# Operands loaded straight into their split buffers, and state space rows in two blocks of 512 columns around the memory tiles

## The chip, the core and the metric

The kernel runs on one core of a Trainium2 chip. The metric is the time of one execution on the device in microseconds (us). A core has a matrix engine (TensorE, PE in the profile; PEld is its weight load), a vector engine (VectorE, DVE), a scalar engine (ScalarE, ACT), a general engine (GpSimd, POOL) and a synchronising engine (SyncE, SP), each with its own instruction queue that is worked off in order. Data moves between the memory of the chip (HBM, "DRAM" in the code) and the on-chip buffers by DMA; this kernel issues its loads on SP's queue and its stores on POOL's. Matmuls write to PSUM, which has eight banks of 128 x 512 float32.

## The reference

One layer of a streaming encoder with 1024 tokens and 1024 features, all in float32. It is three sub-layers, each normalised before and after and added to its input. The change touches the first and the start of the second.

```python
h = rms_norm(x, mix_pre_g)
proj = h @ w_in                       # 512 columns u, 3 x 512 columns q, k, v, 8 gates
y_ssm = s5_mixer(u, ...)              # state space branch, then gelu and a gate
y_fox = forgetting_attention(q, k, v, f_logit)   # 8 heads x 64, causal
y_mix = concatenate([rms_norm(y_ssm, ssm_out_g), rms_norm(y_fox, fox_out_g)])
x = x + rms_norm(y_mix @ w_out, mix_post_g)
h = rms_norm(x, xa_pre_g)
x = x + rms_norm(memory_cross_attention(h, mem_n, xa_wq, xa_wkv, xa_wo), xa_post_g)
h = rms_norm(x, ffn_pre_g)
x = x + rms_norm((silu(h @ w_gate) * (h @ w_up)) @ w_down, ffn_post_g)
```

The cross-attention reads 256 memory tokens (`mem`), with 4 heads of 256; keys and values are `rms_norm(mem) @ xa_wkv`.

## The kernel before

**Products in three parts.** Float32 operands are split into a high part, rounded to the format that PE multiplies fast, and a low part, the rest. `split` (lines 112 to 119) makes both: ACT copies the source to the high part, DVE subtracts it from the source to make the low part. `mm3` (lines 121 to 124) then does three matmuls per product: high x high, high x low, low x high. A weight is loaded into a staging buffer (tag `raw`, two of them, or tag `e`) and split into a pair of tiles (tag `whl`, three of them) by `load_w` (line 154).

**Buffers.** A tag names a set of buffers that are handed out in turn: `slab` (16 of 8 KB per partition), `raw` (2), `whl` (3), `a` (2), `b` (2), `c` (3), `d` and `e` (1 each), `t2` (3 small ones), `yt` (2). A tile's writer waits until the buffer's last user is done. PSUM has four banks tagged `g`; the other four are `s` during attention and `x` behind it.

**Order.** The kernel is traced in Python with generators that hand over to each other, and a scheduler then sets the order of each queue from a model of the times, with priorities by the order of tracing. `tc.issue_after(i)` keeps what is traced inside it behind instruction `i` on that instruction's engine. Nothing is reordered on the chip: a wait at the head of a queue holds what stands behind it.

**Stages.**

1. `in_proj` (line 869): the projections of u, keys, values and queries. Its last part interleaves `v1`, the second half of the value tiles (8 tiles of 24 matmuls), with `ssm_out`, which turns states to outputs; the tuple `V1_AT` says how many value tiles go before each of its steps. Remaining value tiles move on to the next stage.
2. Attention (`fox`, line 705) has 8 heads x 8 query tiles; `paced` takes one step of side work (`fillers`, line 975) behind each of its steps. The side work is in this order: remaining value tiles, the gate (`glu`), one step of the state space rows (`out_ssm`, line 818), the load and split of the memory tokens with five more row steps, sixteen memory tiles (`mem_tile`: one block of 128 columns of `xa_wkv` each, stored to `kv_d`), the remaining rows, and the first two heads' keys times query weights (`build_a(0)`, line 993).
3. `out_ssm` multiplies the state space branch by the upper half of `w_out`, for all 1024 rows, in four blocks of 256 columns. Each block has one split weight tile. Each tile of 128 rows has 4 x 3 matmuls, an evacuation scaled by `r_s` on ACT (line 836), and one store to `t1_d` for two of them (line 840). Its first block computes the row scales (`glu_stats`).
4. Behind attention, lines 1023 to 1082: the lower half of `w_out` is loaded (`raw`) and split into four slabs (line 1026). For each of eight row tiles the kernel loads x (tag `c`, line 1060) and the half result of stage 3 from `t1_d` in two pieces (tags `a`, `a`, `b` in turn, line 1063), multiplies the attention output by the weights, adds the half result (line 1070), squares, scales and adds x (line 1078). `value_weights(0)` and `(1)`, the values times output weights of two memory heads, go between the half tiles. Their values come from `kv_d` through a `t2` buffer (line 1035) into a split tile with tag `b` or `e`.
5. `build_a(1)` and `value_weights(2)` and `(3)`, then the cross-attention and the feed-forward part, which the change doesn't touch.

Of the kernel before, what the change touches and what calls it, by code (L numbers as in the profile page):

```python
# [17 lines left out]
P = 128  # L18
S = 1024
D = 1024  # L20
# [14 lines left out]
MAGIC = 12582912.0  # L35
RATE = 1.02
HP = 16 * (L - 1)
V1_AT = (3, 1, 1, 1, 1)
HID = ("11", "12", "22", "S1", "S2", "S3", "S4")
EVB = 13  # L40
OPB = 10
# [11 lines left out]
def layer(ctx: ExitStack, tc: tile.TileContext, a, out):  # L53
# [24 lines left out]
    def g_ps(shape):  # L78
        return psg.tile(shape, F32, name="g", tag="g")
# [41 lines left out]
    def mm3(ps, lh, ll, rh, rl, first, last):  # L121
        pe.matmul(ps, lh, rh, start=first, stop=False)  # L122
        pe.matmul(ps, lh, rl, start=False, stop=False)  # L123
        pe.matmul(ps, ll, rh, start=False, stop=last)  # L124
# [21 lines left out]
        return last, done  # L146

    boost = 5000
    stA, stB, stC = pool, pool, pool

    def tables(name):
# [2 lines left out]
    def load_w(src, shape, first=0, stage=None):  # L154
        w = tt(stage, [P, D]) if stage else raw([P, D])
        hl = whl([P, 2, D])
        if not first:
            sp.dma_start(out=w, in_=src)
        for cs in (slice(0, first), slice(first, D)):
            if cs.start < cs.stop:  # L160
                if first:
                    sp.dma_start(out=w[:, cs], in_=src[:, cs])
                with tc.high_priority(offset=boost):
                    split(hl[:, 0, cs], hl[:, 1, cs], w[:, cs])
        v = hl.rearrange("p t (a b) -> p t a b", b=shape)
        return v[:, 0], v[:, 1]
# [15 lines left out]
    nc_d = dram.tile([NH, S], F32, name="nc_d")  # L182
    t1_d = dram.tile([L, NC, D], F32, name="t1_d")
    kv_d = dram.tile([16, P, 256], F32, name="kv_d")
    x1_d = dram.tile([NT, P, D], F32, name="x1_d")
    x2_d = dram.tile([NT, P, D], F32, name="x2_d")
    t_d = dram.tile([8, P, 4, 512], F32, name="t_d")
# [7 lines left out]
    def tt(tag, shape=None, dt=F32):  # L195
        return t4.tile(shape or [P, S], dt, name=tag, tag=tag, bufs=BUFS[tag])

    def t2t(shape, dt=F32):
        return tt("t2", shape, dt)
# [616 lines left out]
        rsqrt_mean(r_f, sv, 512)  # L816

    def out_ssm(ys):
        for cc in range(4):
            wh, wl = load_w(a["w_out_s"][cc], 256, stage="e" if cc == 2 else None)  # L820
            for j0 in range(0, NT, 2):
                o = t2t([P, 2, 256])
                made = []
                for j in range(j0, j0 + 2):
                    ts = slice(j * P, (j + 1) * P)
                    ps = g_ps([P, 256])
                    for k in range(4):
                        mm3(ps, ys[k][:, 0, ts], ys[k][:, 1, ts], wh[:, k], wl[:, k], k == 0, k == 3)
                    made.append((j, ps))
                    if cc + j0 == 0:  # L830
                        yield
                        if j == 0:
                            continue
                        glu_stats()
                    for jj, ps in made:
                        act.activation(out=o[:, jj - j0], in_=ps, func=AF.Copy, scale=r_s[:, jj:jj + 1])
                    made = []
                    if j == j0:
                        yield
                stB.dma_start(out=t1_d.rearrange("j c d -> c j d")[:, j0:j0 + 2, cc * 256:cc * 256 + 256], in_=o)  # L840
                yield

    def drain(*gens):
# [25 lines left out]
    def in_proj():  # L869
        r_mem.append(mem_stats())  # L870
        yield from k4
        for i in range(1, 4):
            yield from qk_tile(i + 4, xH, xL, rb)
        for n, _ in enumerate(v_tiles(0, xH, xL, r_x)):
            if n % 2:
                yield
        f_gate(gate[0])
        for i in range(4):
            yield from qk_tile(i, xH, xL, rb)
        drain(gs)  # L880
        go = ssm_out()
        for n in V1_AT:
            step(v1, n)
            step(go)
        drain(go)
# [89 lines left out]
    def fillers():  # L975
        yield from v1
        yield from glu(ys)
        mem = []
        rows = out_ssm(ys)
        step(rows)  # L980
        yield
        for _ in mem_load(r_mem[0], mem):
            step(rows)
            yield
        for i in range(16):
            mem_tile(i, *mem)
            yield
        yield from rows
        yield from build_a(0)
# [3 lines left out]
    def build_a(c):  # L993
        for t in range(2):
            Ah[c, t], Al[c, t] = slab([P, 4, 512]), slab([P, 4, 512])
        for h in range(2):
            hd = 2 * c + h
            kr = t2t([P, 2, 256])
            sp.dma_start(out=kr, in_=kv_d[2 * hd:2 * hd + 2].rearrange("d p m -> p d m"))
            kh = tt(("ea", "ba")[c][h], [P, 2, 2, 256], F32R)  # L1000
            split(kh[:, 0], kh[:, 1], kr)
            wq = [load_w(a["wqT"][2 * hd + d], P) for d in range(2)]
            ms = slice(h * 256, h * 256 + 256)
            for ft in range(0, KT, 2):
                ps = g_ps([P, 2, 256])
                for f in range(2):
                    for d in range(2):
                        mm3(ps[:, f], wq[d][0][:, ft + f], wq[d][1][:, ft + f], kh[:, 0, d], kh[:, 1, d], d == 0, d == 1)
                for f in range(2):
                    split(Ah[c, ft // 4][:, ft % 4 + f, ms], Al[c, ft // 4][:, ft % 4 + f, ms], ps[:, f],  # L1010
                          g_xa[:, ft + f:ft + f + 1])
                yield
# [9 lines left out]

    wo = []
    for i in range(4):
        w = raw([P, D])
        sp.dma_start(out=w, in_=a["w_out_f"][i])
        hl = slab([P, 2, D])
        split(hl[:, 0], hl[:, 1], w)
        wo.append(hl)
    g_mp = gain_row(0, "d")  # L1030
    VW = {}

    def value_weights(h):
        vr = t2t([P, 2, 256])
        sp.dma_start(out=vr, in_=kv_d[8 + 2 * h:8 + 2 * h + 2].rearrange("d p m -> p d m"))
        vh = tt("bebe"[h], [P, 2, 2, 256], F32R)
        split(vh[:, 0], vh[:, 1], vr)
        wo_ = [load_w(a["wo"][2 * h + d], 512) for d in range(2)]
        for mt in range(2):
            VW[2 * h + mt] = slab([P, 2, D])  # L1040
        for c in range(2):
            tiles = [(mt, (x_ps if h == 3 else g_ps)([P, 512])) for mt in range(2)]
            for d in range(2):
                for mt, ps in tiles:
                    ms = slice(mt * P, mt * P + P)
                    mm3(ps, vh[:, 0, d, ms], vh[:, 1, d, ms], wo_[d][0][:, c], wo_[d][1][:, c], d == 0, d == 1)
                    yield
            for mt, ps in tiles:
                split(VW[2 * h + mt][:, 0, c * 512:c * 512 + 512], VW[2 * h + mt][:, 1, c * 512:c * 512 + 512], ps)
# [6 lines left out]
    kept = {}  # L1056
    for n, j in enumerate((3, 4, 5, 6, 7, 0, 1, 2)):
        ts = slice(j * P, (j + 1) * P)
        xt = tt("c")
        sp.dma_start(out=xt, in_=a["x"][ts, :])  # L1060
        t = tt("aab"[n % 3])
        for i in range(2):
            sp.dma_start(out=t[64 * i:64 * i + 64], in_=t1_d.rearrange("j (k s) d -> s k j d", s=16)[2 * j + i])
        ss4, ss, r = sm(4, "ss4"), sm(1, "ss"), sm(1, "r")
        for h in range(2):
            hs = slice(h * 512, h * 512 + 512)
            ps = x_ps([P, 512])
            for k in range(4):
                mm3(ps, yf[k][:, 0, ts], yf[k][:, 1, ts], wo[k][:, 0, hs], wo[k][:, 1, hs], k == 0, k == 3)
            dve.scalar_tensor_tensor(out=t[:, hs], in0=ps, scalar=r_f[:, j:j + 1], in1=t[:, hs], op0=ALU.mult, op1=ALU.add)  # L1070
            for q in range(2 * h, 2 * h + 2):
                act.activation(out=tt("yt", [P, 256]), in_=t[:, q * 256:q * 256 + 256], func=AF.Square,
                               accum_out=ss4[:, q:q + 1])
            pool.tensor_tensor(out=t[:, hs], in0=t[:, hs], in1=g_mp[:, hs], op=ALU.mult)
            step(between)
        dve.tensor_reduce(out=ss, in_=ss4, op=ALU.add, axis=mybir.AxisListType.X)
        rsqrt_mean(r, ss, D)
        dve.scalar_tensor_tensor(out=xt, in0=t, scalar=r, in1=xt, op0=ALU.mult, op1=ALU.add)
        if j < 3:
            kept[j] = xt  # L1080
        else:
            stC.dma_start(out=x1_d[j], in_=xt)
# [489 lines left out]
def lay_out(i):  # L1572
# [11 lines left out]
    def kt(g):  # L1584
# [16 lines left out]
        "ssm_dcol": i["ssm_d"].reshape(4, P).T,  # L1601
        "glu_w": i["ssm_glu_w"].reshape(2, 2, P, 512).transpose(0, 2, 1, 3),
        "glu_b": kt(i["ssm_glu_b"]),
        "w_out_s": i["w_out"][:512].reshape(4, P, 4, 256).transpose(2, 1, 0, 3),
        "w_out_f": i["w_out"][512:].reshape(4, P, D),
        "wkv": cols(i["xa_wkv"]),
        "wqT": i["xa_wq"].T.reshape(8, P, D),
# [21 lines left out]
```

## Time and profile before

| | |
|---|---|
| median of 3 runs | 1413.33 us (1409.28 to 1413.37) |
| the profiled execution | 1414.33 us, span of its instructions 1412.5 us |
| mean granted clock of TensorE | 0.992 |
| PE busy | 1381.8 us (98% of the span) |
| DVE, ACT, POOL busy | 951.9, 652.3, 379.7 us |
| DMA | 239.45 MB, mean 170 GB/s |
| PE without work, 235 to 300 us | 5.1 us of 65 |
| PE without work, 300 to 460 us | 0 of 160 |
| PE without work, 460 to 580 us | 9.0 us of 120 |

An engine is busy from the start to the end of its instructions. Matmuls overlap, so their printed durations add up to more than PE's time, and PE's rate is read from the distance of their starts. "<-" in a row means "written from", and in brackets behind a row stand the idle time before it and what ended it. L122 is line 122 of the kernel. SPq rows are SP's DMA issues. The half results, `t1_d`, appear as `t_d` in the rows.

### The profile page before, as it was taken

Reading aid. Unit: us, or ns where it says so; the run is one execution under the profiler, and the core shown is the slowest. Engines: PE = TensorE matmul, PEld = TensorE weight load, DVE = VectorE, ACT = ScalarE, POOL = GpSimd, SP = SyncE. Lnnn points to the kernel's source line nnn. Section 1 sums busy time; section 2 is a strip of 40 time slices with the busy share of each in tenths; the row PEclk is TensorE's granted clock in tenths of the full one; section 3 lists DMA queues with packets and bytes.
Section 4 is the critical chain, followed back from the end, with each engine's and each line's share of the span. In section 5 each row is a group of like instructions: output and inputs, shape, how many; then the busy total and the mean of one; then the engine's idle time right before and its main releaser. Section 6 shows DMA issues by size and latency. Waiting matters only on the chain.

```text
span 1412.5 us, 20273 instructions
## 1 busy us (share of the span) xinstructions
PE 1381.8 (98%) x7353; PEld 1163.3 (82%) x7353; DVE 951.9 (67%) x1719; ACT 652.3 (46%) x1289; POOL 379.7 (27%) x430
## 2 busy tenths in 40 slices
PE   9999989999999899999999999999999999999997
PEld 7889889789889677888888788888888888888886
DVE  8949944857567668545467777877776676655566
ACT  7383345766566546433344533333333334544351
POOL 0011110011211043001021367676766661000021
PEclk9999999999999999999999999999999999999999
DMA  6235665267663665024467345554444447955544
GB/s 217 91 108 163 201 220 138 69 200 213 183 180 113 175 194 186 27 75 152 161 202 257 97 176 193 178 187 161 145 158 154 165 150 236 357 196 194 179 164 164
DMA packets 104501, 239.45 MB, mean 170 GB/s; under 512 B 11464, under 2 KB 40136, under 8 KB 104272
## 3 DMA queue, kind: packets, MB, share of 16 engines
q1 hardware_dynamic: 85872, 176.24, 40.0%
q0 software_dynamic: 18528, 61.91, 12.3%
q8 instruction: 58, 0.95, 0.3%
q14 instruction: 43, 0.35, 0.1%
HBM read 169.43 MB, written 77.33 MB: 175 GB/s over the span
## 4 chain that ended last, share of the span: by engine, by line
PE 84%; DVE 7%; issue 3%; DMA 3%; ACT 2%; POOL 0%; SPq 0%; DVEq 0%; ACTq 0%; POOLq 0%
PE x L1294 17%; PE g L1294 13%; PE x L1557 7%; PE g L1557 7%; PE g L122 7%; PE g L124 7%; PE g L123 7%; PE x L123 2%; PE x L124 2%; PE g L758 2%; PE x L122 2%; PE g L772 2%; PE s L730 1%; PE s L731 1%; DMA a<-t_d 1%
## 5 line engine op out<-in xcount | busy, mean ns | idle before, releaser
L1294 PE MATMUL x<-slab,op 128*128 128x512 f32 x984 | 233.2, 389 | 0.5 <-DVE op L115 0.5
L1294 PEld LDWEIGHTS x<-slab,op 128*128 128x128 f32 x984 | 184.7, 188 | 39.2 <-DVE op L115 1.0
L1294 PE MATMUL g<-slab,op 128*128 128x512 f32 x744 | 178.7, 389 | 0.0
L115 DVE TENSOR_TENSOR slab<-slab 128x1024 fp32r<-128x1024 f32 (+2 forms) x92 | 110.2, 1207 | 86.4 <-ACT slab L113 85.2
L1294 PEld LDWEIGHTS g<-slab,op 128*128 128x128 f32 x744 | 139.7, 188 | 29.0
L122 PE MATMUL g<-slab,whl 128*128 128x512 f32 (+1 forms) x416 | 151.4, 364 | 0.8 <-ACT slab L485 0.4
L124 PE MATMUL g<-slab,whl 128*128 128x512 f32 (+1 forms) x416 | 148.7, 358 | 0.0
L123 PE MATMUL g<-slab,whl 128*128 128x512 f32 (+1 forms) x416 | 148.3, 357 | 0.0
L113 ACT ACTIVATE slab<-slab 128x1024 fp32r<-128x1024 f32 (+2 forms) x92 | 94.7, 1036 | 108.6 <-DMA slab<-hs_d 80.8
L1557 PE MATMUL g<-slab 128*128 128x512 f32 x462 | 126.6, 389 | 0.0
L1557 PE MATMUL x<-slab 128*128 128x512 f32 x462 | 126.6, 389 | 0.0
L1557 PEld LDWEIGHTS g<-slab 128*128 128x128 f32 x462 | 86.7, 188 | 18.0
L1557 PEld LDWEIGHTS x<-slab 128*128 128x128 f32 x462 | 86.7, 188 | 18.0
L115 DVE TENSOR_TENSOR op<-slab,op 128x512 fp32r<-128x512 f32 x80 | 84.6, 1068 | 11.5 <-ACT op L113 11.3
L1370 POOL TENSOR_TENSOR wt<-wt 128x256 f32<-128x256 f32 x88 | 83.1, 944 | 21.0 <-DMA wt<-in_w_down 17.4
L122 PE MATMUL g<-whl,slab 128*128 128x256 f32 (+2 forms) x288 | 86.8, 310 | 1.7 <-ACT yt L318 0.7
L122 PEld LDWEIGHTS g<-slab,whl 128*128 128x128 f32 x416 | 78.6, 189 | 12.0 <-ACT whl L113 0.6
L124 PEld LDWEIGHTS g<-slab,whl 128*128 128x128 f32 x416 | 78.4, 189 | 11.6 <-DVE whl L115 0.2
L123 PEld LDWEIGHTS g<-slab,whl 128*128 128x128 f32 x416 | 78.6, 189 | 10.6
L113 ACT ACTIVATE op<-slab 128x512 fp32r<-128x512 f32 x80 | 50.0, 628 | 79.9 <-PE g L1294 38.0
L124 PE MATMUL g<-whl,slab 128*128 128x256 f32 (+2 forms) x288 | 86.0, 299 | 0.0
L123 PE MATMUL g<-whl,slab 128*128 128x256 f32 (+2 forms) x288 | 85.7, 298 | 0.0
(397 smaller groups left out, 2890.3 us busy)
## 6 DMA issues: line engine op xcount, KB each, us to landing
hs_d<-ev POOLq DMA_DIRECT2D x77, 256.0 KB, 2.6
slab<-hs_d SPq DMA_DIRECT2D x35, 512.0 KB
wt<-in_w_down SPq DMA_DIRECT2D x44, 256.0 KB
wt_d<-wt POOLq DMA_DIRECT2D x22, 512.0 KB, 5.1
slab<-in_w_gate SPq DMA_DIRECT2D x20, 512.0 KB
slab<-in_w_up SPq DMA_DIRECT2D x20, 512.0 KB
slab<-wt_d SPq DMA_DIRECT2D x20, 512.0 KB
wd_d<-in_w_down SPq DMA_DIRECT2D x33, 256.0 KB
```

Of the source, the lines that this page charges most:

```text
L113: first = act.activation(out=hi, in_=src, func=AF.Copy, scale=1.0 if mul is None else mul)
L115: (lo_eng or dve).tensor_tensor(out=lo, in0=src, in1=hi.bitcast(F32), op=ALU.subtract)
L122: pe.matmul(ps, lh, rh, start=first, stop=False)
L123: pe.matmul(ps, lh, rl, start=False, stop=False)
L124: pe.matmul(ps, ll, rh, start=False, stop=last)
L730: pe.matmul(ps[:, c0:c1], qt, ka[:, 0, c0:c1], start=True, stop=False)
L731: pe.matmul(ps[:, c0:c1], qt, ka[:, 1, c0:c1], start=False, stop=not dg)
L758: pe.transpose(tp[:, k], sc[:, (k0 + k) * P:(k0 + k + 1) * P], ident)
L772: pe.matmul(yp[hh * 64:hh * 64 + 64, c0:], w, pts[2 * hp + hh, qc][:, k, c0:], start=k == 0, stop=k == nk - 1, tile_position=(0, 64 * hh))
L1294: pe.matmul(ps, x[:, k], y[:, k], start=first and k + n == 0, stop=k == 3 and n == 2, skip_group_check=not first)
L1370: pool.tensor_tensor(out=o, in0=x, in1=y, op=ALU.subtract)
L1557: pe.matmul(banks[n][j], xo[:, u, js], wo[:, v], start=ends[0] and k == 0, stop=ends[1] and k == 2, skip_group_check=onto is not None)
```

## The change

- **Rows.** `out_ssm` works in two blocks of 512 columns, each with two split weight tiles, one matmul of 512 columns in place of two of 256, one evacuation and one store per row tile. It hands over twice per row tile, so it has 32 steps (33 before).
- **Order of the side work.** The whole first block (one step and fifteen more) goes with the load of the memory tokens ahead of the sixteen memory tiles; the second block follows them.
- **`V1_AT`** starts with 2 in place of 3: one value tile more is left for attention's side work.
- **In place.** Keys (`build_a`), values (`value_weights`) and the lower half of `w_out` are loaded into the low half of their split tile, which DVE then overwrites with source minus high part. The staging buffers go away there: `t2` for the keys, `raw` for `w_out`. The values' two halves are now two `t2` buffers, in place of a `t2` and a tag `b` or `e`.
- **A copy.** The lower half of `w_out` is copied within HBM to `wof_d` early, on SP behind the last weight load of the keys, and read from there later.
- **Half results and x.** Half results take `a` and `b` in turn (four buffers), x takes `e` for the first and fifth tile and `c` for the others. All loads of x, and the half results of all tiles but the first, are issued behind the last read of `wof_d`.

```diff
-V1_AT = (3, 1, 1, 1, 1)
+V1_AT = (2, 1, 1, 1, 1)
...
     def load_w(src, shape, first=0, stage=None):
...
-            sp.dma_start(out=w, in_=src)
+            fetched.append(sp.dma_start(out=w, in_=src))
...
+    wof_d = dram.tile([4, P, D], F32, name="wof_d")
...
     def out_ssm(ys):
-        for cc in range(4):
-            wh, wl = load_w(a["w_out_s"][cc], 256, stage="e" if cc == 2 else None)
-            for j0 in range(0, NT, 2):
-                o = t2t([P, 2, 256])
-                made = []
-                for j in range(j0, j0 + 2):
-                    ts = slice(j * P, (j + 1) * P)
-                    ps = g_ps([P, 256])
-                    for k in range(4):
-                        mm3(ps, ys[k][:, 0, ts], ys[k][:, 1, ts], wh[:, k], wl[:, k], k == 0, k == 3)
...
-                stB.dma_start(out=t1_d.rearrange("j c d -> c j d")[:, j0:j0 + 2, cc * 256:cc * 256 + 256], in_=o)
+        for c in range(2):
+            ws = [load_w(a["w_out_s"][2 * c + kk], 512) for kk in range(2)]
+            held = []
+            for j in range(NT):
+                ts = slice(j * P, (j + 1) * P)
+                ps = g_ps([P, 512])
+                for k in range(4):
+                    wh, wl = ws[k // 2]
+                    mm3(ps, ys[k][:, 0, ts], ys[k][:, 1, ts], wh[:, k % 2], wl[:, k % 2], k == 0, k == 3)
+                    if k == 1:
                         yield
+                held.append((j, ps))
+                if c + j == 0:
+                    yield
+                    continue
+                if c == 0 and j == 1:
+                    glu_stats()
+                for j_, ps in held:
+                    o = t2t([P, 512])
+                    act.activation(out=o, in_=ps, func=AF.Copy, scale=r_s[:, j_:j_ + 1])
+                    stB.dma_start(out=t1_d[j_][:, c * 512:c * 512 + 512], in_=o)
+                held = []
                 yield
...
         for i in range(1, 4):
             yield from qk_tile(i + 4, xH, xL, rb)
+            if i == 3:
+                with tc.issue_after(fetched[-1].ins):
+                    for j in range(4):
+                        sp.dma_start(out=wof_d[j], in_=a["w_out_f"][j])
...
-        for _ in mem_load(r_mem[0], mem):
+        loads = mem_load(r_mem[0], mem)
+        for _ in range(2 * NT - 1):
+            step(loads)
             step(rows)
             yield
...
-            kr = t2t([P, 2, 256])
+            kh = tt(("ea", "ba")[c][h], [P, 2, 2, 256], F32R)
+            kr = kh[:, 1].bitcast(F32)
             sp.dma_start(out=kr, in_=kv_d[2 * hd:2 * hd + 2].rearrange("d p m -> p d m"))
-            kh = tt(("ea", "ba")[c][h], [P, 2, 2, 256], F32R)
...
-        w = raw([P, D])
-        sp.dma_start(out=w, in_=a["w_out_f"][i])
         hl = slab([P, 2, D])
+        w = hl[:, 1].bitcast(F32)
+        wo_read = sp.dma_start(out=w, in_=wof_d[i])
...
-        vr = t2t([P, 2, 256])
+        vh, vl = t2t([P, 2, 256], F32R), t2t([P, 2, 256], F32R)
+        vr = vl.bitcast(F32)
...
-        vh = tt("bebe"[h], [P, 2, 2, 256], F32R)
-        split(vh[:, 0], vh[:, 1], vr)
+        split(vh, vl, vr)
...
-        xt = tt("c")
-        sp.dma_start(out=xt, in_=a["x"][ts, :])
-        t = tt("aab"[n % 3])
-        for i in range(2):
-            sp.dma_start(out=t[64 * i:64 * i + 64], in_=t1_d.rearrange("j (k s) d -> s k j d", s=16)[2 * j + i])
+        t = tt("ab"[n % 2])
+        with tc.issue_after(wo_read.ins) if n else ExitStack():
+            for i in range(2):
+                sp.dma_start(out=t[64 * i:64 * i + 64], in_=t1_d.rearrange("j (k s) d -> s k j d", s=16)[2 * j + i])
+        xt = tt("ec"[n % 4 > 0])
+        with tc.issue_after(wo_read.ins):
+            sp.dma_start(out=xt, in_=a["x"][ts, :])
...
-        "w_out_s": i["w_out"][:512].reshape(4, P, 4, 256).transpose(2, 1, 0, 3),
+        "w_out_s": i["w_out"][:512].reshape(2, 2, P, 2, 512).transpose(3, 0, 2, 1, 4).reshape(4, P, 1024),
```

More of the change, by code (lines that the diff above doesn't have):

```diff
@@ L148, in layer @@
     boost = 5000
+    fetched = []
     stA, stB, stC = pool, pool, pool
@@ L818, in out_ssm @@
     def out_ssm(ys):
-        for cc in range(4):
-            wh, wl = load_w(a["w_out_s"][cc], 256, stage="e" if cc == 2 else None)
-            for j0 in range(0, NT, 2):
-                o = t2t([P, 2, 256])
-                made = []
-                for j in range(j0, j0 + 2):
-                    ts = slice(j * P, (j + 1) * P)
-                    ps = g_ps([P, 256])
-                    for k in range(4):
-                        mm3(ps, ys[k][:, 0, ts], ys[k][:, 1, ts], wh[:, k], wl[:, k], k == 0, k == 3)
-                    made.append((j, ps))
-                    if cc + j0 == 0:
-                        yield
[L832 to L839, printed above, removed]
-                stB.dma_start(out=t1_d.rearrange("j c d -> c j d")[:, j0:j0 + 2, cc * 256:cc * 256 + 256], in_=o)
+        for c in range(2):
[8 more added lines that the diff above has]
+                    if k == 1:
+                        yield
+                held.append((j, ps))
[9 more added lines that the diff above has]
+                held = []
                 yield
@@ L1045, in value_weights @@
                     ms = slice(mt * P, mt * P + P)
-                    mm3(ps, vh[:, 0, d, ms], vh[:, 1, d, ms], wo_[d][0][:, c], wo_[d][1][:, c], d == 0, d == 1)
+                    mm3(ps, vh[:, d, ms], vl[:, d, ms], wo_[d][0][:, c], wo_[d][1][:, c], d == 0, d == 1)
                     yield
```

## The prediction

> **What bounds the kernel now.** I read the page first (engine shares), then the stretches of the span as a table, then PE's waits, and only at its gaps the order of the instructions, engine by engine.
>
> ```profile
> span 1412.5 us, 20273 instructions
> PE 1381.8 (98%) x7353; PEld 1163.3 (82%) x7353; DVE 951.9 (67%) x1719; ACT 652.3 (46%) x1289; POOL 379.7 (27%) x430
> ```
>
> PE is busy 1381.8 of 1412.5 us, so a change can only shorten PE's work, remove some of its 30.7 us of gaps, or remove the slow clock behind them. The profiled execution took 1414.33 us, 1.8 us more than its span, and the runs shown have a median of 1413.33. I sum against 1414.33 and take 1.0 off at the end. The edits touch what runs between about 105 and 560 us. The gaps there, by stage (columns: stretch, its length, busy time of PE, PEld, DVE, ACT, POOL, the granted clock, DMA share, GB/s):
>
> ```profile
> 190.00:235.00 45.00, 40.54 (x316) 39.41 (x315) 8.16 (x12) 18.41 (x30) 5.55 (x11) 0.92 0.56 169
> 275.00:300.00 25.00, 20.62 (x144) 17.69 (x143) 17.02 (x45) 17.91 (x40) 2.00 (x3) 0.86 0.64 181
> 300.00:365.00 65.00, 65.00 (x535) 59.38 (x533) 41.21 (x79) 37.74 (x74) 9.02 (x16) 1.00 0.63 190
> 485.00:495.00 10.00, 8.46 (x43) 6.34 (x43) 5.06 (x5) 4.92 (x8) 1.72 (x2) 0.83 0.61 191
> 512.00:523.00 11.00, 9.47 (x42) 7.51 (x40) 5.08 (x8) 1.41 (x6) 4.12 (x4) 1.00 0.56 180
> ```
>
> The reader sees two things. From 300 us PE has no gap, so attention's softmax on DVE and ACT is hidden and only PE's own work counts. Elsewhere a gap costs twice: a granted clock of 0.86 over 25 us is 3.5 us of lost work beside the 4.4 us idle, and 0.83 over 10 us is 1.7 us beside 1.5. Who ends the gaps (engine, line, releaser: us, times, longest):
>
> ```profile
> PE g L643 <- ACT t L316: 3.9, 2, 3.3
> PE g L122 <- DVE slab L115: 2.5, 2, 2.0
> PE g L772 <- ACT t L836: 2.4, 1, 2.4
> PE x L122 <- DVE a L1070: 1.9, 1, 1.9
> PE g L758 <- ACT d L782: 1.5, 1, 1.5
> ```
>
> **The wider blocks of state space rows: PE.** The projection of 1024 rows goes from 4x8x4x3 = 384 matmuls of 256 columns to 2x8x4x3 = 192 of 512. What counts is the distance between starts, not the printed duration. Two rows of each width, first and last of an unbroken run (11 and 34 matmuls):
>
> ```profile
> 374.24 0.28 PE L123 MATMUL g<-whl,slab 128*128 128x256 f32 x1
> ...
> 375.43 0.28 PE L124 MATMUL g<-whl,slab 128*128 128x256 f32 x1
> 504.31 0.39 PE L122 MATMUL x<-slab 128*128 128x512 f32 x1
> ...
> 511.79 0.39 PE L122 MATMUL x<-slab 128*128 128x512 f32 x1
> ```
>
> (375.43 - 374.24) / 10 = 0.119 us and (511.79 - 504.31) / 33 = 0.2267 us. So 384 x 0.119 = 45.7 against 192 x 0.2267 = 43.5: **2.2 us less PE work**, in a stage where PE has no gaps, so it counts in full. The Trainium skill (TensorE: Matmul & The Clock Gate, Back-to-back issue gap) gives 2.5 ns on top of the columns for each matmul; by it 192 fewer matmuls are worth an estimated 0.5 us, and the whole sum below would be 1.7 us smaller. The rows show some 12 ns a pair, so the trace doesn't agree, and it decides. On ACT 32 evacuations of 0.47 us become 16 of 512 columns. Their nearest row, a 512-column copy, takes 0.6 to 0.7 us, so ACT saves about 4.7 us, worth nothing by itself beside a PE without gaps. POOL issues as many stores as before.
>
> ```profile
> L836 ACT ACTIVATE t<-g,r_s x32: 450/470/478, 282.3 to 449.9; 128x256 f32<-128x256 f32 x32
> L688 ACT ACTIVATE t<-t x6: 612/617/632, 248.9 to 270.7; 128x512 f32<-128x512 f32 x6
> ```
>
> **The memory tiles move behind the first block.** Before, six row steps and then sixteen memory tiles; after, sixteen row steps, then the tiles. Side work keeps 66 steps, one per attention step. The gap at 287 us:
>
> ```profile
> L115 DVE TENSOR_TENSOR slab<-slab 128x1024 fp32r<-128x1024 f32 (+2 forms) x92 | 110.2, 1207 | 86.4 <-ACT slab L113 85.2
> ...
> 280.12 1.11 SPq L718 DMA_DIRECT2D a<-qk_d  x2
> 281.32 0.53 SPq L158 DMA_DIRECT2D raw<-in_wkv  x1
> 286.22 1.06 ACT L113 ACTIVATE whl<-raw 128x1024 fp32r<-128x1024 f32 x1 [2.22 <-DMA raw<-in_wkv]
> 289.00 0.45 ACT L836 ACTIVATE t<-g,r_s 128x256 f32<-128x256 f32 x1
> 289.51 3.24 PE L772 MATMUL g<-slab 128*64 128x256 f32 x16 [2.37 <-ACT t L836]
> ```
>
> SP is held by attention's query load until 280.12. The first memory weights leave only at 281.32, ACT stands at their split until 286.22, and the evacuation queued behind it releases PE's bank at 289.5. Ten more row steps now lie ahead of that split. The first and the last L836 (282.3 and 449.9, the row above) are 46 steps apart, so a step is 3.6 us and the weights have 36 us more. This takes away 2.4 us and half of this stage's slow-clock loss, 1.7: **-4.1**. The other gap of this stage (1.5 us, L782) hangs on the scale factors, whose place is kept; I leave it and its 1.7, which sets the bounds at 0 and -7.3. In turn block 0 needs two split weight tiles, and the second waits for the gate's weights to be released. A split of 1024 columns is 1.06 us on ACT and 1.2 on DVE (L113 and L115 in the rows), within one step's 3.6: 0, with 2 as the upper bound (no cover).
>
> **One value tile later, V1_AT.** One tile, 24 x 0.119 = 2.9 us, moves into attention's side work; the sum of work stays. The stall there:
>
> ```profile
> 189.63 1.07 POOL L297 DMA_DIRECT2D qk_d<-t  x2 [6.41 <-ACT t L113]
> 198.07 0.47 ACT L316 ACTIVATE t<-g,r_x 128x256 f32<-128x256 f32 x1 [5.92 <-DMA qk_d<-t]
> 198.60 0.80 PE L643 MATMUL g<-slab 128*128 128x128 f32 x2 [3.33 <-ACT t L316]
> ```
>
> The buffer for the second tile's rows comes free when a store issued at 189.63 lands, at 198.07; that isn't moved. PE fills its four banks by then either way. 0; bounds -3.3 (the stall goes) and +2.
>
> **Output weights in place, behind a copy.** The copy is 4 transfers of 512 KB from HBM to HBM, issued on SP after the last key weights (about 101 us). SP is next used at 117.3, and the DMA is empty meanwhile:
>
> ```profile
> 105.00:110.00 5.00, 5.00 (x24) 4.14 (x23) 3.50 (x9) 2.18 (x6) 0.00 (x0) 1.00 0.67 232
> 110.00:115.00 5.00, 5.00 (x29) 4.38 (x28) 5.00 (x11) 1.06 (x1) 0.00 (x0) 1.00 0.00 0
> 100.96 0.80 SPq L158 DMA_DIRECT2D raw<-in_w_f  x2
> 117.30 3.09 SPq L524 DMA_DIRECT2D slab<-slab  x2
> ```
>
> 2 MB at the 232 GB/s of the first row is 9 us: that empty stretch hides it. 0, at most +3 if it slides into the loads of 120 us and later. The reads themselves:
>
> ```profile
> 470.06 3.38 SPq L1060 DMA_DIRECT2D c<-in_x  x2
> 474.52 1.22 SPq L1063 DMA_DIRECT2D a<-t_d  x2
> 475.84 1.23 SPq L1026 DMA_DIRECT2D raw<-in_w_out_f  x2
> 484.41 1.06 ACT L113 ACTIVATE slab<-raw 128x1024 fp32r<-128x1024 f32 x1 [6.41 <-DMA raw<-in_w_out_f]
> ...
> 487.22 2.98 PE L772 MATMUL g<-slab 128*64 128x256 f32 x14 [1.54 <-ACT slab L763]
> ...
> 488.00:489.00 1.00, 1.00 (x9) 0.59 (x6) 0.39 (x1) 0.00 (x0) 0.00 (x0) 0.50 0.80 254
> ```
>
> The last two weights wait for a staging buffer, leave behind two x loads and a half result, and land 8.5 us later. ACT stands at their split for 6.4 us with attention's last evacuations (L763) behind it; PE idles 1.5 us and then has half its clock, 1.7 us of loss. In place they need no staging buffer, and x and all half results but one queue behind them. I take **-3.2**. The Trainium skill (TensorE: Matmul & The Clock Gate, What's actually happening) lets the clock fall after an idle window of about 3.4 us; by it neither this gap nor the one at 287 us costs clock, and the sum below would shrink by 3.4 to -6.2. The last row shows 0.50 right behind a gap of 1.54: the trace does not agree here, so the sum keeps the losses.
>
> **Four buffers for half results; keys and values in place.**
>
> ```profile
> 514.25 3.62 SPq L1063 DMA_DIRECT2D a<-t_d  x4
> 522.53 0.75 DVE L1070 SCALAR_TENSOR_TENSOR a<-x,r_f,a 128x512 f32<-128x512 f32 x1 [5.68 <-DMA a<-t_d]
> ...
> t_d<-t POOLq DMA_DIRECT2D x26, 256.0 KB, 3.2
> ```
>
> A half result leaves at 514.25, when its buffer is free, and lands about 522.5: PE's 1.9 us wait on L1070. With two more choices the load leaves earlier: **-1.9**, or 0 if the queue still holds it. Against it stand the values, which now need two of three small buffers per head, so the second head's load must wait for the first head's products. The load is some 3 us (stores of a like 256 KB land in a median of 3.2), the split about 1.3 by half of the 1024-column rows and their fixed part; half a row tile, 12 x 0.2267 = 2.7 us, covers part. **+1.8**; bounds 0 and 4.5. The keys wait for an attention buffer that is released a head earlier: 0.
>
> **Sum:** -2.2 - 4.1 + 0 + 0 - 3.2 - 1.9 + 1.8 = -9.6; 1414.33 - 9.6 - 1.0 = 1403.7. For gaps that fall elsewhere when five queues are reordered I give back one gap of the kind shown, 1.5 us. **Forecast: 1405 us.**
>
> **The rivals.** *No net change, about 1411.* PE's work falls by 2.2, but the gaps only move: the in-order waits of ACT on a weight split and of DVE on L115 come back at the next load (2.5 us of L122 on L115 stand in the waits). For it: the gaps above end at a wait queued ahead of an unrelated evacuation. Against: DMA is idle or half used around them. *Slower, about 1418: the in-place reads wait for their slabs.* A read into a staging buffer can run ahead; a read into the slab can't leave before attention releases it. If the last slab is one that PE's L772 reads (487.22 + 2.98 = 490.2 in the row above), the read lands 8.5 us later, near 498.7 instead of 484.4, and x and the other half results, tied behind it on SP, later still. PE lacks 14 us of inputs, of which the values' products, 48 x 0.2267 = 10.9, cover half if their own weights are in: 8.5 us idle, 1.7 of clock and 1 for the first half result are +11 in place of -3.2 - 1.9, less the 1.5 and 1.8 already counted: 1405 + 16 - 3 = 1418. It decides once a slab is released later than about 484. Against: rows are worked on from 477 already, so two slabs were free by then. *Larger gain, about 1398:* the scale-factor gap with its clock (-3.2) and the V1_AT stall (-3.3) go too; for it, value tile and evacuations sit in the same queues. *The gaps go, but the clock stays as slow, about 1408:* the slow stretches end and start by themselves and fall on other work; then the 1.7 of the memory term and of the output weights are not won (1405 + 3.4). For it: the 512 to 523 stretch has 1.5 us idle at a clock of 1.00, so a gap need not cost clock. This is also the time by the idle window of the Trainium skill, named above.
>
> **Chances.** Forecast 0.45, clock not won 0.10, larger gain 0.13, no net change 0.19, slower 0.13. Runs within 0.3% (4.2 us) can't be told from no change, so faster means below 1409.1 and slower above 1417.6. Of the forecast 0.03, of the clock case 0.03 and of the slower case 0.01 fall to "same": faster 0.42 + 0.07 + 0.13 = 0.62, same 0.26, slower 0.12. The range runs from just below the larger gain to the slower case's centre: **1396 to 1418**; the forecast's own is 1400 to 1409.
>
> **What would show it.** Right: 192 matmuls of 128x512 at 0.227 us from start to start in the rows; no PE wait on L836 behind a wkv load; 485 to 495 without an idle; no DVE wait of over 2 us on a half result. Wrong: SP's wait ahead of the output weights ends at an attention read and ACT still stands over 5 us at their split; a PE wait at the values' products; PE gaps in 115 to 190.

## The result and the profile after

The changed kernel takes 1417.68 us (median of 6 runs, 1416.81 to 1420.07) against 1409.57 us for the kernel before on the same chip (6 runs, 1405.75 to 1413.37): ratio 1.0055, 95% interval 1.0034 to 1.0075. It is about 8 us slower; 1405 was forecast. The profiled execution took 1418.36 us, its span is 1416.6 us. In the code of the changed kernel, lines up to 145 keep their numbers; behind them L238 is L240, L643 is L645, L763 is L765, L836 is L840, L999 is L1008, L1035 is L1044, L1070 is L1080 and L1078 is L1088. Stretches stand at fixed times, and each edit moves the work by some us against them, so only large differences count.

PE's waits in the changed kernel (engine, line, releaser: us, times, longest):

```profile
PE g L122 <- ACT t L113: 10.8, 1, 10.8
PE g L645 <- DMA slab<-T_d: 2.7, 1, 2.7
PE g L760 <- DVE sv_s L240: 1.8, 1, 1.8
PE g L239 <- ACT slab L765: 1.8, 1, 1.8
PE g L122 <- ACT slab L765: 1.4, 1, 1.4
```

The first is new and is longer than any wait before. By stretch, changed kernel (columns as in the prediction):

```profile
275.00:300.00 25.00, 20.08 (x111) 14.70 (x112) 15.24 (x43) 16.91 (x37) 1.63 (x3) 0.80 0.60 179
485.00:495.00 10.00, 10.00 (x59) 8.36 (x56) 1.77 (x7) 1.37 (x4) 0.74 (x1) 1.00 0.85 204
512.00:523.00 11.00, 10.41 (x46) 8.32 (x45) 9.58 (x18) 6.27 (x23) 6.58 (x6) 1.00 0.92 273
541.00:580.00 39.00, 28.61 (x145) 23.85 (x146) 30.42 (x52) 24.42 (x57) 7.81 (x4) 0.82 0.31 95
```

The last stretch of the kernel before (length, PE busy, granted clock, DMA share, GB/s):

```profile
541.00:580.00 39.00, 35.99 (x192) 0.96 0.39 120
```

The stretch of the output weights, 485 to 495 us, has its full 10 us and full clock. The one at 275 us is no better than before. The loss is behind 541 us: 7.4 us more idle time and a clock of 0.82 in place of 0.96. Read in steps of 0.1 us, the clock is at half from 541.8 to 555.5, but PE has nothing to do until 550.3, so most of that low clock costs no work. The order of events there, engine by engine, in the changed kernel:

```profile
516.26 0.39 SPq L1044 DMA_DIRECT2D t<-kv_d  x1
528.14 0.38 SPq L1008 DMA_DIRECT2D a<-kv_d  x1
544.14 0.38 SPq L1008 DMA_DIRECT2D b<-kv_d  x1
540.40 0.63 ACT L113 ACTIVATE a<-a 128x512 fp32r<-128x512 f32 x1 [10.02 <-DMA a<-kv_d]
546.74 0.63 ACT L113 ACTIVATE b<-b 128x512 fp32r<-128x512 f32 x1 [0.96 <-DMA b<-kv_d]
549.67 0.61 ACT L113 ACTIVATE t<-t 128x512 fp32r<-128x512 f32 x1
541.06 0.69 DVE L115 TENSOR_TENSOR a<-a 128x512 fp32r<-128x512 f32 x1 [10.30 <-ACT a L113]
542.83 1.28 DVE L1088 SCALAR_TENSOR_TENSOR c<-b,r,c 128x1024 f32<-128x1024 f32 x1
550.34 0.80 PE L122 MATMUL g<-whl,t 128*128 128x512 f32 x1 [10.82 <-ACT t L113]
```

These are the keys of the second pair of heads (L1008), loaded in place: the pair's first head into tag b, its second into tag a. The load into a goes first. Tag a comes free only at 528 and the load lands 12.3 us later; ACT stands 10.0 us at its split, and DVE, behind it, 10.3. So DVE gets to the last use of the half result in b (L1088) at 542.83, that buffer is free at 544.1, and only then can the first head's keys leave. ACT splits them at 546.74. Behind both in ACT's queue is the split of the third head's values, whose load had left at 516.26. PE waits 10.8 us for it. It needs the keys themselves later: it multiplies those in b from 558.3 us on, and those in a, which held up ACT first, from 578.8.

The same place in the kernel before:

```profile
454.63 0.41 SPq L999 DMA_DIRECT2D t<-kv_d  x1
526.72 0.38 SPq L999 DMA_DIRECT2D t<-kv_d  x1
542.15 0.63 ACT L113 ACTIVATE b<-t 128x512 fp32r<-128x512 f32 x1 [0.28 <-DVE c L1078]
548.50 0.63 ACT L113 ACTIVATE a<-t 128x512 fp32r<-128x512 f32 x1 [0.95 <-DVE c L1078]
```

The staged loads leave early into t2. By the turn in which its three buffers are handed out, the keys split into b at 542.15 had left at 454.63, and those split into a at 548.50 had left at 526.72. Only the splits wait for b and a, with ACT idle for 0.28 and 0.95 us. The staging buffer took the load's latency out of this wait; in place it is inside it.

### The profile page after: what moved, and what is told of

It reads as the page before. It is cut to its first block, busy times and chain, and to the rows that moved or that the text cites. A ratio compares the mean times of both kernels' runs of the same rounds, so it can differ in the third digit from the quotient of the medians.

```text
span 1416.6 us, 19877 instructions
## 1 busy us (share of the span) xinstructions
PE 1378.3 (97%) x7161; PEld 1150.5 (81%) x7161; DVE 949.1 (67%) x1719; ACT 650.1 (46%) x1273; POOL 377.3 (27%) x430
## 4 chain that ended last, share of the span: by engine, by line
PE 59%; ACT 0%; DVE 0%; DMA 0%; issue 0%; DVEq 0%; ACTq 0%
PE x L1304 17%; PE g L1304 13%; PE x L1567 7%; PE g L1567 7%; PE g L124 2%; PE g L122 2%; PE g L123 2%; PE x L122 2%; PE x L124 2%; PE x L123 2%; PE g L1100 1%; PE g L1211 1%; DMA raw<-in_wqT 0%; ACT whl L113 0%; DVE whl L115 0%
## 5 line engine op out<-in xcount | busy, mean ns | idle before, releaser
L115 DVE TENSOR_TENSOR slab<-slab 128x1024 fp32r<-128x1024 f32 (+2 forms) x96 | 115.1, 1208 | 83.1 <-ACT slab L113 81.6
L113 ACT ACTIVATE slab<-slab 128x1024 fp32r<-128x1024 f32 (+2 forms) x96 | 99.3, 1039 | 103.7 <-DMA slab<-hs_d 78.1
L113 ACT ACTIVATE op<-ss 128x512 fp32r<-128x512 f32 x60 | 37.7, 631 | 91.9 <-PE g L1304 55.7
L115 DVE TENSOR_TENSOR whl<-raw,whl 128x1024 fp32r<-128x1024 f32 (+2 forms) x58 | 64.5, 1118 | 20.9 <-ACT whl L113 20.6
L1407 POOL TENSOR_TENSOR ss<-slab 128x512 f32<-128x512 f32 x40 | 62.2, 1554 | 58.3 <-DMA slab<-in_w_up 25.9
```

The costliest lines, as they stand in the source:

```text
L113: first = act.activation(out=hi, in_=src, func=AF.Copy, scale=1.0 if mul is None else mul)
L115: (lo_eng or dve).tensor_tensor(out=lo, in0=src, in1=hi.bitcast(F32), op=ALU.subtract)
L1407: made[0] = pool.tensor_tensor(out=o, in0=x, in1=y, op=fn)
```

## The experiments

Ratios are to the kernel before, on the same chip and in the same rounds; its medians there were 1410.74, 1411.28 and 1411.86 us (e1 to e4, e5 to e8, e9 to e12). 0.001 is 1.4 us.

| run | edit | median us | ratio, 95% interval |
|---|---|---|---|
| e1 | changed kernel, second keys staged | 1408.85 | 0.9986, 0.9967 to 1.0005 |
| e2 | changed kernel, no order for x and half results | 1419.01 | 1.0057, 1.0038 to 1.0076 |
| e3 | before, second keys in place | 1416.96 | 1.0050, 1.0027 to 1.0073 |
| e4 | before, rows in two blocks around the tiles | 1415.06 | 1.0020, 1.0000 to 1.0039 |
| e5 | e1, first memory split held back | 1406.49 | 0.9967, 0.9951 to 0.9983 |
| e6 | before, output weights and four buffers | 1414.16 | 1.0020, 1.0001 to 1.0039 |
| e7 | before, order of the memory tiles alone | 1412.44 | 1.0002, 0.9982 to 1.0021 |
| e8 | e1, rows as before | 1407.05 | 0.9975, 0.9959 to 0.9991 |
| e9 | before, values in place | 1416.34 | 1.0034, 1.0017 to 1.0052 |
| e10 | before, output weights in place | 1409.63 | 0.9982, 0.9966 to 0.9998 |
| e11 | e5, one value tile back | 1405.82 | 0.9957, 0.9938 to 0.9975 |
| e12 | e8, first memory split held back | 1403.88 | 0.9947, 0.9931 to 0.9963 |

### The second keys: e1, e3, and the rival in e2

Theory 1: the loss is the second pair of keys, in place behind buffers that half results hold. Theory 2: the new order of x and half results clumps their transfers, and the keys' load is only late with them. e1 and e3 share one edit, forward and backward (c is 1 for the second pair of heads):

```diff
+            if c:
+                kr = t2t([P, 2, 256])
+                sp.dma_start(out=kr, in_=kv_d[2 * hd:2 * hd + 2].rearrange("d p m -> p d m"))
             kh = tt(("ea", "ba")[c][h], [P, 2, 2, 256], F32R)
-            kr = kh[:, 1].bitcast(F32)
-            sp.dma_start(out=kr, in_=kv_d[2 * hd:2 * hd + 2].rearrange("d p m -> p d m"))
+            if not c:
+                kr = kh[:, 1].bitcast(F32)
+                sp.dma_start(out=kr, in_=kv_d[2 * hd:2 * hd + 2].rearrange("d p m -> p d m"))
```

e2 takes both `tc.issue_after(wo_read.ins)` away from the loads of x and of the half results.

> The changed kernel with one edit undone: the second pair of key loads (build_a(1)) goes through a small t2 buffer again, as before. Theory 1 (the second keys, read in place into the half results' buffers a and b, leave late, and ACT, DVE, SP and PE queue up behind their split): the 10.8 us PE wait at 539 to 550 us and most of the slow clock behind it (0.82 over 541 to 580, 7 us) go, so about 13 to 17 us less than the changed kernel, 1401 to 1405. Theory 2 (the DMA backlog of deferred x and half results at 512 to 540 us would hold any load there): ACT still stands several us at a key or value split, at most 5 us less, 1413 or more.

> The changed kernel without the order on SP that puts x and half results behind the last read of the output weights; keys and values stay in place. Theory 1: the key load still waits for a half result's buffer and still lands late; the wait at about 540 stays within 3 us of 10.8, the time within 4 us of the changed kernel's. Theory 2: x and half results spread out, the load's 12 us from issue to landing shrink to 4 or less, and 6 to 15 us are gained.

> The kernel before with only the second pair of key loads in place (tags b and a). Theory 1: this edit alone makes a wait of several us at the keys or the values behind them at 540 to 560 us: 5 to 15 us slower than before. Theory 2: without the deferred loads nothing is late: within 3 us of before.

Measured: e1 is 0.0069 below the changed kernel, 9.7 us (uncertain by some 4; e2, in the same rounds, lies 10.0 us above e1), and the 10.8 us wait is gone:

```profile
PE g L122 <- ACT t L113: 2.0, 1, 2.0
...
541.00:580.00 39.00, 35.99 (x209) 1.00 0.27 82
```

(e1: its longest wait in 505 to 580 us, and the stretch.) e2 stays at the changed kernel's time, with a wait of 8.9 us at the same place: the order of x and the half results is not the cause. The load into a takes 11.1 us there as well (526.01 to 537.09), so what makes that load slow stays open. e3 costs 7 us in the kernel before, by the same rows (SP, ACT and PE of e3):

```profile
540.05 0.38 SPq L1004 DMA_DIRECT2D b<-kv_d  x1
544.54 0.63 ACT L113 ACTIVATE b<-b 128x512 fp32r<-128x512 f32 x1 [6.96 <-DMA b<-kv_d]
546.17 0.80 PE L122 MATMUL g<-whl,b 128*128 128x512 f32 x1 [5.15 <-ACT whl L113]
```

Here the load into b goes first and takes only 4.5 us until ACT can split it, and the edit still costs 7 us. So the edit suffices for a loss of this size without a slow load, and taking it out removes the loss. e1 was expected lower, at 1401 to 1405: that counted 7 us of slow clock on top of the wait, and most of the slow clock lay inside the wait.

### Rows and memory tiles: e4, e7, e8, and the held split in e5, e12

e4 takes only the new `out_ssm` with its weights and the order around the tiles; e7 only the order, with blocks of 256 columns (`for _ in range(2 * NT)` around one step of the load and one of the rows); e8 takes both out of e1. e5 and e12 keep the first memory split behind the exponential of its own step:

```diff
-        wh, wl = load_w(a["wkv"][i], P, stage="e" if i % 3 == 2 else None)
+        with ExitStack() if i else behind():
+            wh, wl = load_w(a["wkv"][i], P, stage="e" if i % 3 == 2 else None)
```

> The kernel before with only the state space rows in two blocks of 512 columns around the memory tiles. By the prediction's terms 2.2 us less PE work and 4.1 us from the gap at 287 us: 4 to 7 us faster than before. If the gap only moves: 0 to 2 us faster. In the changed kernel PE idles 4.9 us at 275 to 300 us at a clock of 0.80, which speaks for the second.

> The kernel before with one thing moved: two narrow blocks of state space rows go ahead of the memory tiles, in place of six row steps; blocks stay at 256 columns. By the prediction's term, 4.1 us less (ratio 0.997). By theory A of e5 (the first memory split has a raised priority and stays where it was), no gain at 287 us: 275 to 300 us stays near 20.6 busy and the ratio is 0.999 to 1.002. If it is slower by 2 us or more, the order costs something by itself, which would also be in e4, where rows in two blocks gave 1.002.

> The changed kernel with the second pair of keys staged and with the state space rows and the memory tiles as before: what is left are output weights, half results, first keys and values in place and the value tile. If the rows bring 2.2 us of PE work, this is 2 us slower than e1 (ratio to before 1.000). If they bring nothing, as e4 says, it is as e1 or up to 4 us faster (ratio 0.996 to 0.9986), and against e6 it shows what first keys, values and the value tile cost together: the prediction says +1.8.

> The changed kernel with the second pair of keys staged, as in e1, and the split of the first memory weights kept behind the exponential of its own step. Theory A: the memory term of the prediction failed because that split has a raised priority and still stands at 285 us; held back, ACT evacuates PE's banks there earlier, the wait of 1.4 to 2.1 us on L765 before 287 us goes, 275 to 300 us is busy for 21.5 us or more (e1: 19.98) at a clock above 0.85, and the time is 2 to 4 us below e1's (1408.9 there): 1405 to 1407. Theory B: the gaps there come from the row scales alone (table load, sv_s, L239), and the split is only what stands there: 275 to 300 us stays at 20 busy, and the time within 1.5 us of e1.

> e8 (second keys staged, rows and memory tiles as before) with the split of the first memory weights kept behind the exponential of its own step. Theory A: as in e5, 275 to 300 us becomes busier or its clock higher (e8: 22.98 at 0.77), 2 to 3 us less than e8: ratio 0.995 to 0.9965. If so it ties with e5, and the wider rows bring at most their 2.2 us of PE work; if e5 stays 2 us below this one, they bring that. Theory B: no difference to e8 (0.9975 within 0.001).

Measured: the order alone is worth nothing that can be told (1.0002, uncertain by 0.002). The changed kernel suggests why:

```profile
281.38 0.33 SPq L159 DMA_DIRECT2D raw<-in_wkv  x1
284.84 1.06 ACT L113 ACTIVATE whl<-raw 128x1024 fp32r<-128x1024 f32 x1 [0.71 <-DMA raw<-in_wkv]
323.98 1.04 ACT L113 ACTIVATE whl<-raw 128x1024 fp32r<-128x1024 f32 x1
...
279.76 1.05 PE L239 MATMUL g<-ones,d 128*128 128x1 f32 x8 [1.78 <-ACT slab L765]
283.85 1.33 PE L760 MATMUL g<-ident,c 128*128 128x128 f32 x5 [1.79 <-DVE sv_s L240]
286.53 0.80 PE L122 MATMUL g<-whl,slab 128*128 128x512 f32 x1 [1.35 <-ACT slab L765]
```

The first memory weights are loaded and split at 281 and 285 us as before, 39 us ahead of the second ones. By the code, `load_w` gives its splits a raised priority (line 164), and one of the three weight buffers was free; taking the priority away was not tried by itself. In e7 the first memory split comes at 292.96 us, only 7 us later than before. Held back, the first split brings 2.7 us (e1 to e5) and 4.0 us (e8 to e12). That is near the prediction's 4.1, but each difference is uncertain by some 3 us, so the first could be nothing. The split moves from 282 to 323 us in e5, and only from 282 to 287 in e12. In e12 275 to 300 us is busy for 24.61 us at a clock of 0.86 (e8: 22.98 at 0.77). In e5 275 to 300 us is busy for 20.97 us at a clock of 0.86, a little short of the 21.5 expected: the waits for the row scales (L239, L760) stand as in e1, which is theory B's part of it.

Wider rows did not pay in any of three pairs: e4 against e7 is 0.0018 slower, e1 against e8 0.0011, e5 against e12 0.0020 (the last two pairs include the order of the tiles). No pair alone is past its uncertainty of 3 to 4 us, but none shows the expected gain of 2.2 us. The matmuls themselves did get cheaper (changed kernel, an unbroken run):

```profile
296.66 0.39 PE L123 MATMUL g<-whl,slab 128*128 128x512 f32 x1
...
298.95 0.39 PE L124 MATMUL g<-whl,slab 128*128 128x512 f32 x1
```

(298.95 - 296.66) / 10 = 0.229 us, so 45.7 - 192 x 0.229 = 1.7 us less work. But in e4 the stage that had no gap has 4.2 us of them (300 to 460 us; the middle stretch is busy throughout):

```profile
300.00:365.00 65.00, 63.56 (x493) 1.00 0.71 207
365.00:420.00 55.00, 55.00 (x384) 1.00 0.56 163
420.00:460.00 40.00, 37.26 (x258) 1.00 0.40 123
```

The longest waits in these rows are for weight splits (1.5 us, tag e) and for evacuations (L971, 1.4 us), while the blocks hold two of the three split weight buffers. That this holding is the cause was not tried by itself. At 275 to 300 us, on the other hand, e4 is busy for 23.14 us at full clock, better than before: here the gaps moved. This profiled execution took 1410.02 us, 5 us less than the median of e4, so it shows where gaps can come and not the whole loss.

### Output weights, buffers, values: e10, e6, e9

e10 takes the copy, the reads in place and the order of x and half results, with the old tags; e6 adds the four buffers (`t = tt("ab"[n % 2])`, `xt = tt("ec"[n % 4 > 0])`); e9 takes the values alone (`vh, vl = t2t(...), t2t(...)`).

> The kernel before with the output weights copied in HBM, read in place, and x and half results issued behind them; half results and x keep their buffers (a, a, b and c). By the prediction's term, 3.2 us less: ratio 0.9977, and 485 to 495 us without idle time at a clock of 1.00. Theory C: the 2.9 us by which e6 was slower come from the four buffers beside the values' tiles, so without them the ratio is 0.997 to 0.9995 and no wait of PE on L1078 is above 2 us. If the ratio is 1.001 or more, the reads in place or their order cost by themselves.

> The kernel before with three parts only: the output weights copied in HBM and read in place, x and half results issued behind them, and four buffers for half results. Keys, values, rows and the value tiles stand as before. By the prediction's terms, 3.2 + 1.9 less: ratio 0.9964, some 5 us below the kernel before, with 460 to 541 us busy for 79 us of 81 (before: 75.05). By the rival that gaps only move: ratio 0.999 to 1.001, with the idle time back behind 541 us or in the copy's stretch (100 to 190 us).

> The kernel before with one part only: the values loaded in place into two t2 buffers, their split tiles no longer in tags b and e. Half results keep their three buffers. By the prediction's term, 1.8 us more (0 to 4.5): ratio 1.0013. Theory C: this part pays only together with the four buffers for half results, because the values' split tiles held b and e, the very buffers that half results and x take now (e6, which has four buffers without it, shows a 5.5 us wait of PE on the half result in b); alone it is worth nothing: ratio 0.999 to 1.001, and PE's wait on the half result near 520 us stays at 1 to 2 us. If it is 3 us or more faster by itself (ratio below 0.998), the values carry the gain of e8 over e6 alone.

Measured: the output weights alone gain 2.5 us, and their stretch in e10 is full; the copy's is as full as before (88.91):

```profile
485.00:495.00 10.00, 10.00 (x68) 7.95 (x65) 1.98 (x3) 1.14 (x4) 2.46 (x2) 1.00 0.80 226
100.00:190.00 90.00, 88.90 (x571) 78.21 (x570) 85.20 (x176) 37.15 (x71) 12.87 (x24) 1.00 0.62 185
```

Four buffers on top cost 5.4 us (e10 to e6, uncertain by 3.5), values in place alone 4.8 us (e9). With both, and the first keys and the value tile, e8 is 1.0 us below e10, uncertain by some 3. So either costs alone, and together they don't. The rows suggest why. In e6 the values' split tiles still take b and e by the code, and PE multiplies the first head's values out of b until 495.7 us; the second half result for b leaves at 506.00, the third at 512.64, and DVE and PE wait for it (SP, DVE, PE):

```profile
506.00 1.20 SPq L1068 DMA_DIRECT2D b<-t_d  x2
...
512.64 1.21 SPq L1068 DMA_DIRECT2D b<-t_d  x2
517.32 1.41 DVE L1078 SCALAR_TENSOR_TENSOR b<-x,r_f,b 128x512 f32<-128x512 f32 x2 [6.72 <-DMA b<-t_d]
518.13 0.79 PE L122 MATMUL x<-slab 128*128 128x512 f32 x1 [5.54 <-DVE b L1078]
```

In e8 the second one leaves 29 us sooner (SP):

```profile
475.12 1.22 SPq L1072 DMA_DIRECT2D b<-t_d  x2
476.38 0.92 SPq L1075 DMA_DIRECT2D c<-in_x  x2
477.35 1.22 SPq L1072 DMA_DIRECT2D b<-t_d  x2
```

In e9 half results are still late, and the split of the third head's values stands behind them on ACT. In the kernel before it stood at 525.02, into a buffer b; why it comes 27 us later here was not tried (SP, DVE, ACT, PE):

```profile
538.09 3.61 SPq L1063 DMA_DIRECT2D a<-t_d  x4
546.30 0.75 DVE L1070 SCALAR_TENSOR_TENSOR a<-x,r_f,a 128x512 f32<-128x512 f32 x1 [1.97 <-DMA a<-t_d]
547.09 0.42 ACT L1072 ACTIVATE yt<-a 128x256 f32<-128x256 f32 x1 [3.59 <-DVE a L1070]
552.29 0.62 ACT L113 ACTIVATE t<-t 128x512 fp32r<-128x512 f32 x1
552.96 0.79 PE L122 MATMUL g<-whl,t 128*128 128x512 f32 x1 [7.02 <-ACT t L113]
```

### The value tile: e11

The edit is `V1_AT = (3, 1, 1, 1, 1)` again.

> e5 (second keys staged, first memory split held back) with V1_AT starting at 3 again. By the prediction's term 0: within 1.5 us of e5 (ratio 0.9956 to 0.9978). 100 to 190 us should be busy for 88.9 of 90 again (e5: 87.36), and 190 to 235 us for less than e5's 42.4. If it is 2 us or more slower, the tile moved into attention pays by the stall at 198 us.

Measured: 0.9957 against 0.9967, no difference that can be told. 100 to 190 us is busy for 88.91 again and 190 to 235 us for 40.51 of 45: the idle time changes its side of 190 us. 275 to 300 us is busy for 24.08 us at full clock here (e5: 20.97 at 0.86), and the time is still the same: a stretch that looks better in one trace is not yet a gain.

## Why the prediction was wrong, point by point

The time lies at the upper end of the stated 1396 to 1418 us, but faster was forecast and the kernel is slower.

- **"The keys wait for an attention buffer that is released a head earlier: 0."** This is the step that failed: put at 0, it cost 9.7 us (e1), with a wait of 10.8 us on PE. It holds for the first pair of heads only. The second pair takes tags b and a behind the half results, and the load in place can't leave before the last half result is done with its buffer. The prediction named what waits for slabs and for small buffers, and didn't follow tags a and b to their last user.
- **Memory tiles, -4.1.** Measured 0 (e7). "Ten more row steps now lie ahead of that split" was read from the order of tracing, but the split stayed at 285 us, most likely by its raised priority. The price of the gap was about right: 2.7 and 4.0 us when the split is held back (e5, e12), each uncertain by some 3.
- **Wider rows, -2.2.** PE's work fell by 1.7, but "no gaps, so it counts in full" was a state of the kernel before: between 300 and 460 us the changed kernel is idle for 1.3 us and e4 for 4.2. The middle of the three pairs is 2.5 us of loss, uncertain by more than that; a gain of 2.2 is not in any.
- **Output weights, -3.2.** Right: -2.5, uncertain by 2.2 (e10), with 485 to 495 us full, and the copy hidden.
- **Four buffers -1.9, values +1.8.** Right as a sum (-1.0 measured with first keys and value tile, e8 against e10), wrong as two terms: alone they are +5.4 and +4.8. Whether one pays depends on the other. In the changed kernel DVE waits for no half result from 455 to 580 us (before: 6.6 us) and PE's wait on L1070 is gone, as forecast.
- **V1_AT, 0.** Right (e11).
- **The sum again,** from these runs: -2.5 - 1.0 + 1.6 (rows and order in place, e1 against e8) + 9.7 = +7.8 us, the measured 8. These are the steps from the kernel before over e10, e8 and e1 to the changed kernel, so they must add up; the sum shows that 9.7 of it is the keys, and does not check the steps.
- **The rivals.** "Slower, about 1418" has the time by luck and not the mechanism: the output weights' reads cost PE nothing, and a price like its 8.5 us idle and 1.7 us of clock came at the second keys, another in-place read behind a late buffer. No net change is what is left without the keys (e1: 0.9986). Of the signs of being wrong, "a PE wait at the values' products" came, and "PE gaps in 115 to 190" too: that stretch is busy for 72.14 us of 75 (before: 74.33). By e10 and e11 the copy is not what does it, but the value tile, and 190 to 235 us gives most of it back (42.17 against 40.54).

A version that beats both kernels is e12: the change without its second keys, its rows and its order, with one split held back, 0.9947 (0.9931 to 0.9963), some 7.5 us below the kernel before. With its rows (e5) it is still faster than the kernel before: 0.9967.

## What to carry to other kernels

A staging buffer is not only a copy of space: it lets a load leave before its destination is free, and in place the whole latency of the load comes behind the release. Follow each buffer of an in-place load to its last user before costing it at nothing, for every call of the function, and follow whoever is queued behind the split. Edits that free a buffer and edits that use it are priced together, and where a scheduler sets the order, look in the trace whether a step moved in the code has moved on the chip.

## What the runs showed of the hardware

Behind two long gaps PE runs at half its clock for some 5 us. In the changed kernel behind 10.8 us of idle time:

```profile
550.93 0.63 PE L123 MATMUL g<-whl,t 128*128 128x512 f32 x1
...
554.77 0.63 PE L124 MATMUL g<-whl,t 128*128 128x512 f32 x1
555.20 0.52 PE L122 MATMUL g<-whl,t 128*128 128x512 f32 x1
```

(554.77 - 550.93) / 9 = 0.427 us a matmul against 0.227, from 550.3 to 555.2 us: 12 matmuls by 0.2 are 2.4 us. In e6, behind 5.5 us, the half clock lasts from 518.1 to about 523.0. The Trainium skill (TensorE: Matmul & The Clock Gate, What's actually happening) has a cold clock after an idle window of about 3.4 us. These two gaps are longer, but in the first the clock fell 2.3 us after PE ran dry (541.8 against 539.5). The changed kernel's stretch at 286 us does not agree: three gaps of at most 1.79 us within 9 us, 4.9 in all, and the clock is down to half as well, from 282.4 us, early in the second gap, to 292.7:

```profile
286.00:292.00 6.00, 5.47 (x14) 3.89 (x14) 3.49 (x10) 3.84 (x8) 1.08 (x2) 0.50 0.62 187
```

How long the clock stays low can't be read from the gap. In steps of 0.1 us it is low for 10.2 us there, for 13.7 around the 10.8 us gap (541.8 to 555.5), for 6.8 in e6 (516.4 to 523.2) and for 3.4 in the kernel before behind its gap of 1.54 us (487.5 to 490.9). These are 3, 4, 2 and 1 times 3.4 us, so in these traces the clock is held in steps of that length. What makes it fall was not tried.

The load of 256 KB that left at 528.14 took 12.3 us until ACT could read it, in a stretch where the DMA share was 0.84. The pair's other load, of the same size, took 2.6 us (544.14 to 546.74), and loads of 256 KB elsewhere land in a median of 3.5 us. In e2 the load took 11.1 us at a share of 0.71 (526 to 537 us), so the share alone does not tell the time, and the cause is open (changed kernel, the stretch and the list of DMA issues):

```profile
528.00:540.00 12.00, 11.52 (x51) 9.20 (x49) 2.28 (x6) 1.01 (x5) 3.09 (x3) 1.00 0.84 260
```

```profile
wt<-in_w_down SPq DMA_DIRECT2D x44, 256.0 KB, 3.5
```
